# One layer of a hybrid decoder trunk: index queries of rows 64 to 255 alone, index keys in passes of 512 columns

## The chip, the core and the metric

The kernel runs on one core of a Trainium2 chip, as one launch. The metric is the device time of that launch in microseconds (us), as the median of several executions. One more execution was taken with the hardware profiler; all rows of the profile come from it.

## The reference, cut to what matters

One layer works on x (256 rows, 1024 features). After an RMS norm, one projection gives the inputs of a convolution branch and of an attention branch whose keys are chosen by an index:

```python
n = RMSNorm(x)
c_a, c_g, q, k, v, qi, ki, wi, gc, ga = split(n @ w_in)   # qi 8 heads x 64, ki 64, wi 8
# index: per block of 128 query rows
logits = einsum('qhd,sd->qhs', qi, ki) * 64**-0.5
score  = einsum('qh,qhs->qs', wi * 8**-0.5, relu(logits))
score  = where(key <= row, score, -inf)
idx    = top_k(score, 64)              # k_top = min(256, 256 // 4)
s      = q . k[idx], -inf where idx > row ; softmax ; times v[idx]
h = x + W_mix(g_conv * Conv(n) + g_attn * Attn(n))
h = h + CrossAttn(RMSNorm(h), RMSNorm(mem))
h = h + W2 relu(W1 RMSNorm(h))^2 ; final RMSNorm
```

A row r has r + 1 keys that it may look at. Rows 0 to 63 have at most 64 of them, so that the choice of 64 takes all, whatever the scores are. Only rows 64 to 255 need index queries.

## The kernel before

**Number format.** Every large product is made in float32 precision from two parts of each operand: a high part (rounded by ScalarE, `act(hi, raw, Copy)`) and a low part (the rest, `raw - hi`, by VectorE). Three products are kept: high by high, high by low, low by high. The activations of a tile lie as high and low beside each other, 256 columns each. A *wide* tile (`tile_b` with `wide=True`) therefore makes, for each of 8 blocks of features, one pass of 512 columns with the high weights (high and low activations at once) and one pass of 256 columns with the low weights. The two halves of the PSUM bank are then merged: ScalarE copies the second half out, VectorE adds the first (`merge`, L479). A tile that is not wide makes three passes of 256 columns and needs no merge. `back` alternates the order in which neighbouring tiles make their wide and narrow passes.

**Order of the work.** All engines follow one order, written out by the program itself; each engine's queue is first in, first out. `STREAM` lists the weight chunks (1 MB each) in the order of use: four `conv` chunks, two `qi` chunks (four tiles of 128 index query features), `ki` (64 key features and the 8 head weights `wi`, 72 columns), four more `conv` chunks, the gates `gc` and `ga`, then `v`, `q` and `k`, the memory's `xk` and `xv`, then `ao`, `co`, `mix`, the cross attention and the feed-forward part. Chunks are fetched on SyncE's queue into three buffers; a buffer comes free when VectorE has made the second low part.

**The planner.** After every tile of products `tick()` (L373) emits one step of each running chain (generators such as `memory`, `merge`, `index_scores`, `head`, `layer_norm`), then as many *fill* operations as the planner allows, then perhaps one `add_some`. Fill operations are VectorE's convolution taps (31 shifts per tile of 128 channels) and the rounds of the top-64 choice. The planner adds up prices in ns of its own: a pass of n columns costs `pe.total` n/2.4; a VectorE operation costs `dve.total` n/0.96 + 70, or + 125 with a scalar by pointer. It emits fill operations while `dve.total < pe.total - 1000` (L377). When all taps of a tile are out, `settled(t)` adds the tile to `usum` and to `done`; when eight are done, the chain `layer_norm` is started. It makes its first step at the *next* tick. One step per tick it emits the means (`ps_mub`), squares, sums (`ps_vr`), the spread of the root (`ps_rsb`), and then, per pair of channel tiles, a multiplication (VectorE), two Silu and a copy (ScalarE, L912 and L913) and the low part (VectorE, `parts_of`), which comes one step after the copy. Its result `u_p` is the input of `co`, which follows `ao` on TensorE.

**Taps by DMA.** Some taps are made by ScalarE (`products`, L714) and added to `acc` by an accumulating DMA that POOL issues (`add_tap`, L715). `add_some` emits the first one at the first tick after `conv` chunk 3, the next when `pe.total` has grown by a pause of 5000. Each of these DMAs adds into the same region, and each waits on POOL for the one before it to land.

**Index.** `qi_t` holds the four tiles of index queries (features by 256 rows). `ki2` (a part of `picked`) holds the keys twice, `wi_t` the head weights. `index_scores` is started after the key tile: at the tick after the first tile of `conv` chunk 4 it transposes `wi_t` (`ps_wi`) and emits the 16 passes of query block 0 (`ps_idx`), which read rows 0 to 127 of `qi_t` for all four tiles. TensorE reaches them behind that `conv` tile.

**Memory.** The chain `memory` squares the memory rows, has POOL take the root `rs_m` (L629), has TensorE spread it over the partitions (two transposes, `ps_mrb`) for ScalarE to copy into `mrb`, and then splits `mem_t` into parts, one of 8 per tick. `mrb` is used much later, in `residual`.

Of the kernel before, what the change touches and what calls it, by code (L numbers as in the profile page):

```python
# [8 lines left out]
F32 = mybir.dt.float32  # L9
F32R = mybir.dt.float32r  # L10
BF16 = mybir.dt.bfloat16
AF = mybir.ActivationFunctionType
ALU = mybir.AluOpType
# [3 lines left out]
P = 128  # L17
D = 1024
S = 256
KT = D // P  # L20
# [3 lines left out]
HD = 128  # L24
XH = 4
K_TOP = 64
IDX_SCALE = float((8 ** -0.5) * (64 ** -0.5))
ATT_SCALE = float(HD ** -0.5)
NEG_FILL = -1.0e38
NEG_TAKEN = -3.4e38  # L30
NEG_BIAS = -1.0e30
# [23 lines left out]
NK = 72  # L55
# [36 lines left out]
class Parts:  # L92
# [5 lines left out]
    def of(self, part, kt, n):  # L98
        t = self.tiles[kt // 4][:, kt % 4 : kt % 4 + n, part, :]
        return t[:, 0, :] if n == 1 else t  # L100

    def high(self, kt, n=1):
        return self.of(0, kt, n)
# [18 lines left out]
def block_kernel(ctx, tc, x, xt, mem, memt, wst, wki, vecs, convw, gout, out):  # L122
    nc = tc.nc
    ctx.enter_context(tc.manual_schedule())
    pe = Counted(nc.tensor, pe_price)
    dve = Counted(nc.vector, dve_price)
    act = nc.scalar.activation
# [5 lines left out]
    lows = ctx.enter_context(tc.tile_pool(name="lows", bufs=HALVES))  # L133
# [4 lines left out]
    def t8(name, dt=F32, shape=(P, KT, S)):  # L138
        return big.tile(list(shape), dt, tag="t8", bufs=12, name=name)
# [4 lines left out]
    def w2(name, dt=F32, shape=(P, 512)):  # L144
        return work.tile(list(shape), dt, tag="w2", bufs=8, name=name)
# [13 lines left out]
    def ps_aux(name):  # L159
        return bank("aux", 2, name)  # L160
# [3 lines left out]
    def ps_turn(name):  # L164

        mm_turn[0] += 1
        return (ps_mm if mm_turn[0] % 2 else ps_acc)(name)
# [156 lines left out]
    def split_high():  # L324
        if high_jobs and high_jobs[0].here() and (not high_jobs[0].slot or nsplit[0] - nused[0] < HALVES - held[0]):
            job = high_jobs.pop(0)
            nsplit[0] += job.slot
            while job.steps:
                job.step()
            job.high()  # L330
# [9 lines left out]
    nsplit, nused, held = [0], [0], [1]  # L340

    def weights(kind, i, half, kt):

        key = (kind, i, half)
        while key not in prepared:
            split_high()
            split_low()
        nused[0] += key not in elsewhere
        return [w if kt is None else w.rearrange("p (k n) -> p k n", k=kt) for w in prepared.pop(key)]


    chains, fours, fill, turn, done, ended = [], [], [], [0], [], []
# [16 lines left out]
    def split_ahead():  # L369
        split_low()  # L370
        split_high()

    def tick():  # L373
        for c in list(chains):
            if next(c, "end") == "end":
                chains.remove(c)
        while (len(fill) > 1 or (fill and (len(ended) > 5 or nused[0] < 5))) and dve.total < pe.total - 1000:  # L377
            fill_one()
        if fours and next(fours[0], "end") == "end":
            fours.clear()  # L380
        dve.total = max(dve.total, pe.total - 2000)
        add_some()
# [14 lines left out]
    def start(gen):  # L397
        chains.append(gen)
        return gen
# [10 lines left out]
    def mm_b(ps, wh, wl, x2, kt, start, stop):  # L410
        mm3(ps, wh, wl, x2.high(kt), x2.low(kt), start, stop)

    def tile_b(ps, w, x2, kts=range(KT), wide=False, late=False, back=False):

        ps = ps[: w[0].shape[2]]

        def lows(last):  # L420
            for kt in kts:
                pe.matmul(ps[:, S:], w[1][:, kt, :], x2.high(kt), start=False, stop=last and kt == KT - 1)

        if wide and not late:
            for kt in kts:
                pe.matmul(ps, w[0][:, kt, :], x2.both(kt), start=kt == 0, stop=back and kt == KT - 1)
                if back and kt == 0:
                    lows(False)
            if not back:
                lows(True)  # L430
            return
        for kt in kts:
            wh, wl = w[0][:, kt, :], w[1][:, kt, :]
            if not wide:
                mm_b(ps[:, :S], wh, wl, x2, kt, kt == 0, kt == KT - 1)
            elif kt == 0:
                pe.matmul(ps, wh, x2.both(kt), start=True, stop=False)
                pe.matmul(ps[:, S:], wl, x2.high(kt), start=False, stop=False)
            else:
                pe.matmul(ps[:, S:], wl, x2.high(kt), start=False, stop=False)  # L440
                pe.matmul(ps, wh, x2.both(kt), start=False, stop=kt == KT - 1)

    back = [False]

    def is_wide(kind, ct):

        return kind in ("f1", "qi", "gc", "ga", "ao", "xk", "q", "k") or (kind in ("mix", "co") and ct < 6)

    def form_b(kind, i, x2, after, ps_of=ps_mm):

        for ct in range(2):
            w = weights(kind, i, ct, KT)
            if (kind, i, ct) != ("mix", 3, 1):
                split_ahead()
            ps = ps_of(f"ps_{kind}{i}{ct}")
            wide = is_wide(kind, 2 * i + ct)
            tile_b(ps, w, x2, wide=wide, back=back[0])
            back[0] = wide and not back[0]
            after(2 * i + ct, ps if wide else ps[:, :S])
            tick()  # L460
# [24 lines left out]
    def merge_now(dst, ps):  # L485
        for _ in merge(dst, ps):
            pass
# [9 lines left out]
    def copy_to(dst):  # L497
        return lambda ct, ps: copy_out(dst[:, ct, :], ps)
# [27 lines left out]
    picked = w4("picked", F32, (P, D))  # L526
    ki2 = picked[:, 3 * S :]
# [3 lines left out]
    ps = ps_aux("ps_warm")  # L531
# [22 lines left out]
    def spread(cols, name):  # L554

        ps = ps_aux(f"ps_{name}")
        for rb in range(2):
            pe.transpose(ps[:, rb * P : rb * P + P], cols[:, rb : rb + 1].to_broadcast([P, P]), ident)
        return ps[:, :S]


    n2 = parts_t8("n_p")
# [8 lines left out]
    for rb in range(2):  # L571
        for kt in range(KT):
# [5 lines left out]
                             in1=x_rm[:, 1, D // 2 :], scale=1.0 / D, scalar=EPS, op0=ALU.mult, op1=ALU.add,  # L578
# [21 lines left out]
    for lo, hi in ((0, 1), (1, 2), (2, 4), (4, 6), (6, 8)):  # L600
        dve.tensor_tensor(out=n_f[:, lo:hi, :], in0=xg[:, lo:hi, :],
                          in1=rsb_n.unsqueeze(1).to_broadcast([P, hi - lo, S]), op=ALU.mult)
# [10 lines left out]
    rs_m = cst.tile([P, 2], F32, name="rs_m")  # L613
    mrb = cst.tile([P, S], F32, name="mrb")

    def memory():
        mem_rm = t8("mem_rm", F32, (P, 2, D))
        mem_t = t8("mem_t")
        nc.sync.dma_start(mem_rm, mem.rearrange("(r p) d -> p r d", p=P))
        nc.sync.dma_start(mem_t, memt)  # L620
        yield
        yield
        yield
        ss = small.tile([P, 2], F32, tag="ss", name="ss_m")
        for rb in range(2):
            row_square(mem_rm, rb, ss)
            yield
        dve.tensor_scalar(ss, ss, 1.0 / D, EPS, ALU.mult, ALU.add)
        nc.gpsimd.tensor_tensor(out=rs_m, in0=ss, in1=half, op=ALU.pow)  # L629
        yield  # L630
        act(mrb, spread(rs_m, "mrb"), AF.Copy)
        for kt in range(KT + 1):
            if kt < KT:
                act(mem2.high(kt), mem_t[:, kt, :], AF.Copy, scale=g_mem[:, kt : kt + 1])
            if kt > 0:
                j = kt - 1
                dve.scalar_tensor_tensor(out=mem2.low(j), in0=mem_t[:, j, :], scalar=g_mem[:, j : j + 1],
                                         in1=mem2.high(j).bitcast(F32), op0=ALU.mult, op1=ALU.subtract)
            yield


    u = t8("u")
# [123 lines left out]
            start(memory())  # L766


    qi_t = t8("qi_t", F32, (P, 4, S))
    for i in range(2):  # L770
        form_b("qi", i, n2, copy_to(qi_t), ps_turn)
    wk = weights("ki", 0, 0, KT)
    split_ahead()
    ps = ps_mm("ps_ki")
    tile_b(ps, wk, n2)
    for j in range(2):
        act(ki2[j * 64 : j * 64 + 64, :], ps[:64, :S], AF.Copy)
    wi_t = w2("wi_t", F32, (P, S))
    act(wi_t[64:NK, :], ps[64:NK, :S], AF.Copy, scale=IDX_SCALE)
    tick()  # L780
    wi = cst.tile([P, 2, 8], F32, name="wi")

    bias = [picked[:, :P], picked[:, P : 3 * P]]
# [6 lines left out]
    def choose(qb, score):  # L790

        def turn(r):
            def go():
                m8 = small.tile([P, 8], F32, tag="m8", name=f"m8_{qb}_{r}")
                dve.max(out=m8, in_=score)
                dve.match_replace(out=score, in_to_replace=m8, in_values=score, imm_value=NEG_TAKEN)
                dve.total += 250
            return go

        def mask():  # L800
            dve.tensor_scalar(bias[qb], score, -3.3e38, NEG_BIAS, ALU.is_gt, ALU.mult)
            causal(bias[qb], qb, NEG_BIAS)

        return [turn(r) for r in range(K_TOP // 8)] + [mask]

# [417 lines left out]
    dst = open_banks("xo")  # L1223
    w = weights("xo", 0, 0, 1)
# [9 lines left out]
    w = weights("xo", 0, 1, 1)  # L1234
# [259 lines left out]
    for c in range(JOINED):  # L1494
        hidden.append(Hidden(c + 2))
        x, later = hidden[c], hidden[c + 2]
        wide = c in WIDE
# [134 lines left out]
```

## Time and profile before

| | |
|---|---|
| median of 3 runs | 497.05 us (496.95 to 497.06) |
| the profiled execution's own time | 497.16 us |
| its span in the profile | 495.0 us |
| TensorE (PE) busy | 487.3 us, 98% |
| VectorE (DVE) busy | 460.5 us, 93% |
| ScalarE (ACT) busy | 378.4 us, 76% |
| GpSimd (POOL) busy | 50.6 us, 10% |
| TensorE clock granted | 0.998 |

Times in the rows are us from the start of the span. PE is a matmul pass, PEld its weight load, SP the engine that issues most DMAs. A busy TensorE counts passes that overlap in its pipeline, so that the distance between the starts of two passes in a row, not the length of one, is what a pass costs.

### The profile page before, as it was taken

How to read it: one execution, taken by the hardware profiler on the slowest of the kernel's cores; microseconds unless marked ns; L12 is line 12 of the kernel's file. 1: busy time of each engine (PE TensorE's matmuls, PEld its weight loads, DVE VectorE, ACT ScalarE, POOL GpSimd, SP SyncE). 2: the span in 40 equal slices, each digit the busy share in tenths (PEclk: the TensorE clock that was granted, in tenths of full speed). 3: DMA queues.
4: the chain of work that ended last, by engine and by line, in shares of the span. 5: the costliest groups of instructions: out<-in, count | busy, mean ns of one | idle time of the engine just before them, and what ended most of it. 6: DMA issues, size and time to landing. Idle time of an engine off the chain costs nothing.

```text
span 495.0 us, 7793 instructions
## 1 busy us (share of the span) xinstructions
PE 487.3 (98%) x2832; PEld 429.2 (87%) x2832; DVE 460.5 (93%) x828; ACT 378.4 (76%) x678; POOL 50.6 (10%) x67
## 2 busy tenths in 40 slices
PE   8999999999999999999999999999999999999995
PEld 7888888888888889888889999988998888888884
DVE  4999999999999989989988987899999999999986
ACT  5778879999887786767846558687777878888852
POOL 2002212221111211000000000000010101121000
PEclk9999999999999999999999999999999999999999
DMA  8958676989887977354645552866979879999802
GB/s 318 354 215 276 180 190 198 304 245 253 277 219 223 246 176 213 115 171 175 250 169 183 209 204 87 290 189 138 253 274 292 237 242 262 294 333 314 256 9 85
DMA packets 33430, 110.36 MB, mean 223 GB/s; under 512 B 11104, under 2 KB 13408, under 8 KB 24432
## 3 DMA queue, kind: packets, MB, share of 16 engines
q1 hardware_dynamic: 24416, 93.03, 54.4%
q0 software_dynamic: 8688, 16.64, 17.2%
q8 instruction: 22, 0.36, 0.3%
q10 hardware_dynamic: 288, 0.20, 0.1%
q14 instruction: 16, 0.13, 0.1%
HBM read 99.29 MB, written 1.05 MB: 203 GB/s over the span
## 4 chain that ended last, share of the span: by engine, by line
PE 97%; DVE 1%; issue 0%; ACT 0%; DVEq 0%
PE ps_f L87 18%; PE ps_p L87 15%; PE ps_conv L87 9%; PE ps_co L87 5%; PE ps_mix L87 5%; PE ps_ao L87 5%; PE ps_k L87 5%; PE ps_ga L87 5%; PE ps_gc L87 5%; PE ps_q L87 5%; PE ps_v L87 4%; PE ps_xo L87 3%; PE ps_xq L87 2%; PE ps_xk L87 2%; PE ps_qi L87 2%; PE ps_xv L87 2%
## 5 line engine op out<-in xcount | busy, mean ns | idle before, releaser
L87 DVE TENSOR_TENSOR lo<-raw,hi 128x1024 fp32r<-128x1024 f32 x133 | 161.3, 1215 | 2.5 <-ACT hi L315 2.2
L315 ACT ACTIVATE hi<-raw 128x1024 fp32r<-128x1024 f32 x133 | 138.5, 1048 | 6.2 <-DMA raw<-in_wst_dram 6.1
L87 PE MATMUL ps_f<-ff_p,hi 128*128 128x512 f32 (+1 forms) x320 | 72.4, 347 | 0.0
L87 PEld LDWEIGHTS ps_f<-ff_p,hi 128*128 128x128 f32 x320 | 56.2, 189 | 8.2 <-ACT ft L1344 0.3
L87 DVE SCALAR_TENSOR_TENSOR acc<-u,cw,acc 128x241 f32<-128x241 f32 (+23 forms) x142 | 58.5, 465 | 0.1
L87 PE MATMUL ps_f<-ff_p,lo 128*128 128x256 f32 x256 | 46.8, 282 | 0.0
L87 PEld LDWEIGHTS ps_f<-ff_p,lo 128*128 128x128 f32 x256 | 39.3, 191 | 1.8
L715 POOL DMA_DIRECT2D acc<-products x25 | 21.7, 880 | 124.2 <-ACT products L714 59.5
L87 PE MATMUL ps_conv<-n_p,hi 128*128 128x512 f32 x112 | 29.2, 397 | 0.0
L87 PEld LDWEIGHTS ps_conv<-n_p,hi 128*128 128x128 f32 x112 | 20.4, 188 | 4.4 <-issue 0.3
L714 ACT ACTIVATE products<-u,cw 128x243 f32<-128x243 f32 (+19 forms) x50 | 22.1, 492 | 0.0
L293 ACT ACTIVATE inner<-sums 128x1024 fp32r<-128x1024 f32 x13 | 13.8, 1060 | 10.5 <-DVE sums L87 10.5
L87 DVE TENSOR_TENSOR ft<-ft 128x128 f32<-128x128 f32 (+2 forms) x49 | 19.4, 397 | 1.1 <-ACT ft L1344 0.6
L683 ACT ACTIVATE ring<-u,cw 128x236 f32<-128x236 f32 (+10 forms) x44 | 20.2, 480 | 0.0
L87 PE MATMUL ps_p<-outer,fs 128*128 128x512 f32 x78 | 20.1, 393 | 0.0
L87 PE MATMUL ps_v<-hi,n_p 128*128 128x512 f32 x64 | 19.9, 389 | 0.0
L87 PE MATMUL ps_p<-inner,fs 128*128 128x512 f32 x78 | 19.8, 389 | 0.0
L87 PE MATMUL ps_co<-u_p,hi 128*128 128x512 f32 (+1 forms) x80 | 19.3, 350 | 0.0
L87 PE MATMUL ps_mix<-mix_p,hi 128*128 128x512 f32 (+1 forms) x80 | 19.2, 349 | 0.0
L87 PE MATMUL ps_k<-n_p,hi 128*128 128x512 f32 x64 | 17.4, 403 | 0.0
L87 PE MATMUL ps_q<-n_p,hi 128*128 128x512 f32 x64 | 17.3, 402 | 0.0
L87 PEld LDWEIGHTS ps_p<-inner,fs 128*128 128x128 f32 x78 | 14.6, 188 | 3.0
(445 smaller groups left out, 1215.0 us busy)
## 6 DMA issues: line engine op xcount, KB each, us to landing
raw<-in_wst_dram SPq DMA_DIRECT2D x67, 1024.0 KB, 5.7
raw<-in_wst_dram SPq DMA_DIRECT2D x28, 512.0 KB, 6.7
sums<-in_wst_dram POOLq DMA_DIRECT2D x15, 512.0 KB, 8.0
acc<-products POOLq DMA_DIRECT2D x25, 256.0 KB, 5.5
x_rm<-in_x_dram SPq DMA_DIRECT2D x2, 512.0 KB, 4.0
mem_rm<-in_mem_dram SPq DMA_DIRECT2D x1, 1024.0 KB, 7.6
mem_t<-in_memt_dram SPq DMA_DIRECT2D x1, 1024.0 KB, 9.6
h_t<-in_xt_dram SPq DMA_DIRECT2D x1, 1024.0 KB, 7.0
```

The costliest lines, as they stand in the source:

```text
L87: return fn(*args, **kwargs)
L293: act(hi, src, AF.Copy)
L315: act(hi, raw[:, ns], AF.Copy)
L683: act(dst[:, t, :], u[:, 4 * g + t, : S - s], AF.Copy, scale=cw[:, 4 * g + t, TAPS - 1 - s : TAPS - s])
L714: act(prod[:, a, s:], u[:, t, : S - s], AF.Copy, scale=cw[:, t, TAPS - 1 - s : TAPS - s])
L715: nc.gpsimd.dma_start(acc[:, ts, :], prod, accum_op=ALU.add)
```

## The change

1. The four `qi` tiles are made by a new function `tile_behind` for rows 64 to 255 alone: wide passes of 2 x 192 = 384 columns and narrow passes of 192. `query_part` merges 192 columns.
2. POOL sets rows 0 to 63 of `qi_t` to zero, and the first 64 rows of the bias of block 0 (`picked`). Both memsets stand behind the `qi` loop, ahead of the key tile. `mask` leaves those 64 rows of the bias alone.
3. The key tile becomes wide: 8 passes of 512 columns and 8 of 256 in place of 24 of 256. It is merged at once into `wi_t`, from which ScalarE then makes `ki2` and the head weights. `back` is turned over behind it, so that all later wide tiles up to `co` alternate the other way round.
4. The spread of the memory's root and its copy to `mrb` move to the end of the chain `memory`, nine ticks later.
5. The planner's distance of 1000 becomes 0 from the tick on at which four tiles are `done`.

```diff
+FREE = K_TOP
+    def behind(self, kt, row):
+        return self.tiles[kt // 4][:, kt % 4, :, row:]
@@ tick
-        while (len(fill) > 1 or (fill and (len(ended) > 5 or nused[0] < 5))) and dve.total < pe.total - 1000:
+        while (len(fill) > 1 or (fill and (len(ended) > 5 or nused[0] < 5))) and dve.total < pe.total - (1000 if len(done) < 4 else 0):
             fill_one()
+    def tile_behind(ps, w, x2, row, back=False):
+        both = ps.rearrange("p (a n) -> p a n", a=2)
+        def lows(last):
+            for kt in range(KT):
+                pe.matmul(both[:, 1, row:], w[1][:, kt, :], x2.high(kt)[:, row:], start=False, stop=last and kt == KT - 1)
+        for kt in range(KT):
+            lo = row
+            pe.matmul(both[:, :, lo:], w[0][:, kt, :], x2.behind(kt, lo), start=kt == 0, stop=back and kt == KT - 1)
+            if back and kt == 0:
+                lows(False)
+        if not back:
+            lows(True)
@@ memory
         yield
-        act(mrb, spread(rs_m, "mrb"), AF.Copy)
         for kt in range(KT + 1):
             ...
             yield
+        act(mrb, spread(rs_m, "mrb"), AF.Copy)
@@ the index queries and keys
-    for i in range(2):
-        form_b("qi", i, n2, copy_to(qi_t), ps_turn)
+    def query_part(dst, ps):
+        both = ps.rearrange("p (a n) -> p a n", a=2)[:, :, FREE:]
+        act(dst, both[:, 1, :], AF.Copy)
+        yield
+        dve.tensor_tensor(out=dst, in0=both[:, 0, :], in1=dst, op=ALU.add)
+    for ct in range(4):
+        w = weights("qi", ct // 2, ct % 2, KT)
+        split_ahead()
+        ps = ps_turn(f"ps_qi{ct}")
+        tile_behind(ps, w, n2, FREE, ct % 2 == 1)
+        start(query_part(qi_t[:, ct, FREE:], ps))
+        tick()
+    assert not back[0]
+    nc.gpsimd.memset(qi_t[:, :, :FREE], 0.0)
+    nc.gpsimd.memset(picked[:FREE, :P], 0.0)
     wk = weights("ki", 0, 0, KT)
     split_ahead()
     ps = ps_mm("ps_ki")
-    tile_b(ps, wk, n2)
+    tile_b(ps, wk, n2, wide=True)
+    back[0] = True
+    wi_t = w2("wi_t", F32, (P, S))
+    merge_now(wi_t[:NK, :], ps[:NK, :])
     for j in range(2):
-        act(ki2[j * 64 : j * 64 + 64, :], ps[:64, :S], AF.Copy)
-    wi_t = w2("wi_t", F32, (P, S))
-    act(wi_t[64:NK, :], ps[64:NK, :S], AF.Copy, scale=IDX_SCALE)
+        act(ki2[j * 64 : j * 64 + 64, :], wi_t[:64, :], AF.Copy)
+    act(wi_t[64:NK, :], wi_t[64:NK, :], AF.Copy, scale=IDX_SCALE)
     tick()
@@ mask
-            dve.tensor_scalar(bias[qb], score, -3.3e38, NEG_BIAS, ALU.is_gt, ALU.mult)
+            rows = slice(0 if qb else FREE, P)
+            dve.tensor_scalar(bias[qb][rows], score[rows], -3.3e38, NEG_BIAS, ALU.is_gt, ALU.mult)
```

## The prediction, made before the changed kernel was timed

> **What bounds the kernel now.** I read the page's busy times first, then what TensorE (PE) waited for, then the chain that ended last, in order of time.
>
> ```profile
> PE 487.3 (98%) x2832; PEld 429.2 (87%) x2832; DVE 460.5 (93%) x828; ACT 378.4 (76%) x678; POOL 50.6 (10%) x67
> PE ps_warm L533 <- DVE zero_r L517: 1.9, 1, 1.9
> ```
>
> PE is the bound, and it waited once, 1.9 us, before its first pass. From there the chain is PE alone until the last products:
>
> ```profile
> 31.96 8.34 PE ps_qi L87 x48
> 40.29 0.38 PE ps_mrb L87 x2
> 40.67 2.80 PE ps_qi L87 x16
> 43.47 2.82 PE ps_ki L87 x24
> 46.29 2.78 PE ps_conv L87 x16
> 49.07 0.22 PE ps_wi L87 x2
> 49.28 1.09 PE ps_idx L87 x16
> ...
> 168.85 0.33 PE ps_pt L87 x3
> ...
> 219.05 0.43 PE ps_mub L87 x2
> ...
> 231.09 0.22 PE ps_rsb L87 x2
> 231.31 11.16 PE ps_ao L87 x64
> 242.47 22.57 PE ps_co L87 x144
> ```
>
> So each pass that goes is worth its distance to the next, and each new wait of PE costs in full. The profiled execution took 497.16 us, 0.11 above the median of the runs, 497.05; I work on the former and take 0.11 off at the end. A measurement of this kernel tells about 0.2% (1.0 us) from no change.
>
> **The narrower queries.** A run of narrow passes and one of wide ones give the prices.
>
> ```profile
> 33.61 1.12 PE L87 MATMUL ps_qi<-n_p,lo 128*128 128x256 f32 x8
> 34.56 0.40 PE L87 MATMUL ps_qi<-n_p,hi 128*128 128x512 f32 x1
> ...
> 35.75 3.59 PE L87 MATMUL ps_qi<-n_p,hi 128*128 128x512 f32 x15
> 39.18 1.11 PE L87 MATMUL ps_qi<-n_p,lo 128*128 128x256 f32 x8
> ```
>
> Start to start, eight narrow passes take 34.56 - 33.61 = 0.95, 0.119 each; 15 wide ones 39.18 - 35.75 = 3.43, 0.229 each. 256 columns thus cost 0.110, 128 cost 0.055. The 32 wide passes lose 128 columns each: 1.76 us. The narrow ones lose 64, which the slope puts at 0.0275, down to 0.091; but a pass of only 128 columns still takes 0.33 / 3 = 0.110 (`ps_pt`), so there is a floor under short passes. A 192-column pass lies between 0.091 and 0.119; the nearest row says 0.110, which saves 32 x 0.009 = 0.28 us (ends 0 and 0.9).
>
> **Keys.** 24 passes took 2.82 us, 0.1175 each. Eight of 512 and eight of 256 columns take 8 x 0.229 + 8 x 0.1175 = 2.77: 0.05 saved. **The root's spread** cost 0.38 where it stands, since its transposes waited for POOL; the like pair `ps_rsb` costs 0.22. It saves 0.38 ahead of the index products and pays 0.22 back later; its nine ticks of delay meet nobody, as `mrb` is read in `residual` only. The other order of wide and narrow passes behind the keys leaves their number as it is: nothing (some 0.1 either way).
>
> Without new waits PE would reach `ps_idx` 1.76 + 0.28 + 0.38 + 0.05 = 2.47 us sooner, at 49.28 - 2.47 = 46.8, and the gain left after the spread is 2.25.
>
> **New wait at the index products: the zeros.** `ps_idx` of block 0 reads rows 0 to 127 of `qi_t`, so it now needs POOL's memset. What stands ahead of that in POOL's queue?
>
> ```profile
> 7.57 0.29 POOL L708 MEMSET products<- 128x248 f32 x1
> 38.20 0.91 POOL L715 DMA_DIRECT2D acc<-products  x1 [30.33 <-ACT products L714]
> 38.84 1.35 POOL L629 TENSOR_TENSOR rs_m<-ss_m,half 128x2 f32<-128x2 f32 x1
> 47.72 0.91 POOL L715 DMA_DIRECT2D acc<-products  x1 [7.53 <-ACT wi_t L779]
> 53.67 0.86 POOL L715 DMA_DIRECT2D acc<-products  x1 [5.04 <-DMA acc<-products]
> ```
>
> The second accumulating DMA stood 7.53 us in front of a closed gate. The releaser named is ScalarE's `wi_t`, which it doesn't read. Its own input was long there, and the first DMA landed just then:
>
> ```profile
> 36.74 0.86 ACT L714 ACTIVATE products<-u,cw 128x236 f32<-128x236 f32 x2
> 41.66 0.87 ACT L714 ACTIVATE products<-u,cw 128x237 f32<-128x237 f32 x2
> ...
> acc<-products POOLq DMA_DIRECT2D x1, 256.0 KB, 9.0
> ```
>
> 38.20 + 9.0 = 47.2, and 0.5 later POOL goes on. Where is the second DMA emitted after the change? The first is emitted at the tick after the first `qi` tile and sets the next due 5000 planner ns later. A `qi` tile now counts 8 x 576 / 2.4 = 1920: after the third it has 3840, after the fourth 5760. So the second DMA goes out at the fourth tile's tick, still **ahead of the memsets**, and the zeros stand behind a wait for the first DMA's landing. The first starts at the same time as before, since ScalarE, busy with earlier work, makes its input at 36.74, two microseconds after the PE tile. If it lands at 47.2 again: second DMA at 47.7, next POOL operation 0.64 behind it (as 38.84 behind 38.20), memset 0.29, done at 48.65; the second memset is read much later. `ps_idx` then starts at 48.7, not at 46.8: PE waits 1.9 us, and of the 2.25 gained 0.35 is left. PE can do nothing else there, its queue is in order.
>
> The landing sets this price alone. Over all 25 of these DMAs, and for the third alone:
>
> ```profile
> DMA to landing us min/median/max: 3.4/5.5/10.0
> ...
> acc<-products POOLq DMA_DIRECT2D x1, 256.0 KB, 3.7
> ```
>
> At 10.0 the kernel is 0.6 slower at this point; at 7.1 or less the zeros come in time (7.1 + 1.5 + 38.2 = 46.8). The weight chunks that compete are fetched when VectorE frees a buffer, and with fewer taps emitted in this stretch that is sooner, so more traffic, not less, meets this DMA. I take 9.0 again.
>
> The merged keys put a VectorE addition into the chain to `wi_t`. From the key tile's last pass (46.29 - 2.47 = 43.8): copy 0.38, addition 0.42, two copies and `wi_t`:
>
> ```profile
> 46.33 0.77 ACT L777 ACTIVATE picked<-ps_ki 64x256 f32<-64x256 f32 x2 [1.23 <-PE ps_ki L87]
> 47.11 0.38 ACT L779 ACTIVATE wi_t<-ps_ki 8x256 f32<-8x256 f32 x1
> 45.94 1.22 DVE L87 TENSOR_TENSOR lo<-raw,hi 128x1024 fp32r<-128x1024 f32 x1
> ```
>
> That is 1.95 with handoffs some 2.3, at 46.1; PE asks at 46.6. If VectorE is inside a weight split of 1.22, PE waits up to 0.7, but that lies under the wait for the zeros: nothing.
>
> **New wait ahead of `co`: one tick.** Fewer planned PE ns mean fewer taps emitted by any given tick: 32 x (128 + 64) / 2.4 = 2560 less, VectorE 70 more (an addition of 337, four merges 67 shorter). The new distance gives 1000 back from the fourth finished tile on; 1630 stays missing. I added up the kernel's own prices in the order of emission: before, at the tick after the third `xv` quarter, `pe.total` is 193,947 and `dve.total` 192,085, and the last two fill operations (337 each, the `usum` additions) go out, the last started at 192,422 under a limit of 192,947. With the change the limit is 193,947 - 2560 = 191,387, and the last would start at 192,492. It misses by 1105, three taps. The remaining fill goes out one tick later, and `layer_norm` makes its first step after the first `ao` tile instead of ahead of it. In the trace its end is tight:
>
> ```profile
> 216.29 0.87 DVE L87 TENSOR_TENSOR usum<-usum,acc 128x256 f32<-128x256 f32 x2
> 240.14 0.68 DVE L87 TENSOR_TENSOR acc<-acc,ps_rsb 128x512 f32<-128x512 f32 x1
> 243.27 0.69 DVE L87 TENSOR_TENSOR u_p<-acc,u_p 128x512 fp32r<-128x512 f32 x1
> ...
> 240.85 1.09 ACT L912 ACTIVATE acc<-acc,vec 128x256 f32<-128x256 f32 x2
> 241.98 0.63 ACT L913 ACTIVATE u_p<-acc 128x512 fp32r<-128x512 f32 x1
> ...
> 244.42 0.28 PE L87 MATMUL ps_co<-u_p,lo 128*128 128x256 f32 x1
> 244.54 0.62 PE L87 MATMUL ps_co<-u_p,hi 128*128 128x512 f32 x2
> ```
>
> The last low part ends at 243.96; PE's seventh wide pass of `co` needs it at 244.54. An `ao` tile with its tick is (242.47 - 231.31) / 4 = 2.79. One tile later the copy ends at 242.61 + 2.8 = 245.4. The low part now follows it at once (before, a weight split lay between): 246.1. PE waits 246.1 - 244.5 = 1.6. Ends: 0 if the shift doesn't come, 2.2 if the low part moves by the whole tile.
>
> **Sum.** -2.25 + 1.9 + 1.6 = +1.25: 497.16 + 1.25 - 0.11 = 498.3. Everything else that is added (mask of fewer rows, VectorE's addition of 0.42) lies on engines that PE doesn't wait for.
>
> **The rivals.**
> *The zeros are in time; only the tick costs.* This needs the first accumulating DMA to land within 7.1 us of its start. For it: the median of the 25 is 5.5, and the third took 3.7. Against it: the one in this place took 9.0 between weight chunks. Time: 497.05 - 2.25 + 1.6 = 496.4, not slower. The Trainium skill, "DMA: Bandwidth & Descriptors", section on the anatomy of one DMA, fits a POOL-issued transfer as 2.0 us plus its bytes over 436 GB/s, which for 256 KB is an estimated 2.6 us; by that rule this rival wins. The row above, 9.0 in this place and never under 3.4, disagrees with the rule, so I trust the row.
> *The zeros cost, the tick does not:* `co` has more room than I read, say because ScalarE, with one step less ahead of it, runs sooner. 497.05 - 0.35 = 496.7.
> *Neither:* the change does what it seems to, 497.05 - 2.25 = 494.8, 494.2 if the narrow passes follow the slope down to 0.091.
> *The narrow passes don't get shorter:* alone it changes nothing, as PE only waits less for the zeros.
>
> **How the numbers follow.** Both waits: 0.60, at 498.3 (own range 497.4 to 499.4, from a landing of 8.5 to 10.0 us and 1.2 to 2.2 at `co`). Tick alone 0.15, zeros alone 0.12, neither 0.13. Leaving out "neither" and the far end of the first case, the range is 495.6 to 499.4. Slower means over 498.0: 0.6 of the first case, 0.36. Faster means under 496.06: most of "neither", a third of "tick alone" and little else, 0.20. Within: 0.44.
>
> **What would show it.** Right: `ps_qi` wide passes start every 0.174 us and narrow ones near 0.110; PE's list of waits has POOL's `qi_t` (1 to 2.5 us) ahead of `ps_idx`, with a memset directly behind a waiting DMA issue; `ps_mub` stands behind the first `ao` tile and PE waits for `u_p` inside `co`. Wrong: the memset is done before the first `conv` tile behind the keys ends, or `ps_mub` still stands ahead of `ao`.

## The result and the profile after

The changed kernel took 500.28 us (median of 14 executions, 498.42 to 508.4), the kernel before 497.12 (14 executions, 496.92 to 502.68). The ratio of the two is 1.0063, with a 95% interval of 1.0035 to 1.009: slower, by more than the 0.2% that can be told. Medians here and below are over all executions; the ratios and their intervals leave out the executions furthest above the rest, and are not the ratios of these medians. The profiled execution took 499.72 us with a span of 497.9 (before: 497.16 and 495.0), and its mean granted clock was 0.994 (before: 0.998).

The page's busy times and TensorE's list of waits (us in total, times, longest) of the changed kernel:

```profile
PE 486.5 (98%) x2824; PEld 428.9 (86%) x2824; DVE 460.8 (93%) x829; ACT 378.8 (76%) x679; POOL 52.7 (11%) x69
PE ps_idx L88 <- POOL qi_t L806: 3.2, 1, 3.2
...
PE ps_mub L88 <- DVE usum L88: 0.2, 1, 0.2
```

TensorE's narrower passes should have taken some 2 us off its busy time; only 0.8 is gone. And one wait of 3.2 us is new. TensorE's timeline of the changed kernel (start, us, group) shows both places:

```profile
33.17 1.03 PE L88 MATMUL ps_qi<-n_p,lo 128*128 128x192 f32 x8
34.04 0.36 PE L88 MATMUL ps_qi<-n_p,hi 128*128 128x384 f32 x1
...
35.11 2.78 PE L88 MATMUL ps_qi<-n_p,hi 128*128 128x384 f32 x15
37.73 1.03 PE L88 MATMUL ps_qi<-n_p,lo 128*128 128x192 f32 x8
...
46.60 0.28 PE L88 MATMUL ps_wi<-ident,wi_t 8*128 8x8 f32 x2
50.13 1.16 PE L88 MATMUL ps_idx<-picked,qi_t 64*128 64x128 f32 x16 [3.25 <-POOL qi_t L806]
51.22 3.68 PE L88 MATMUL ps_conv<-n_p,hi 128*128 128x512 f32 x8
54.74 1.11 PE L88 MATMUL ps_conv<-n_p,lo 128*128 128x256 f32 x8
```

Start to start, 15 wide passes take 37.73 - 35.11 = 2.62, 0.175 each, and eight narrow ones 34.04 - 33.17 = 0.87, 0.109 each. `ps_wi` ends at 46.88, so that TensorE was ready for `ps_idx` 2.40 us sooner than the 49.28 of before. Then it stood 3.25 us. The eight `conv` passes behind that start 3.52 / 8 = 0.44 us apart, where passes of 512 columns had been 0.229 apart.

POOL's timeline says what it stood for:

```profile
38.13 0.91 POOL L735 DMA_DIRECT2D acc<-products  x1 [30.22 <-ACT products L734]
38.77 2.09 POOL L649 TENSOR_TENSOR rs_m<-ss_m,half 128x2 f32<-128x2 f32 x1
48.84 0.91 POOL L735 DMA_DIRECT2D acc<-products  x1 [7.98 <-ACT sg L501]
49.43 0.65 POOL L806 MEMSET qi_t<- 128x256 f32 x1
```

The zeros stand behind the second accumulating DMA, whose issue stood 7.98 us. The chain of work that ended last, of the changed kernel and then of the kernel before (start, length, what), gives the reason and the account:

```profile
38.13 10.17 DMA acc<-products
50.13 1.16 PE ps_idx L88 x16
51.29 10.12 PE ps_conv L88 x48
...
72.31 0.22 PE ps_mrb L88 x2
...
75.31 22.29 PE ps_gc L88 x128
...
221.88 0.70 PE ps_mub L88 x2
222.58 8.37 PE ps_ao L88 x48
...
245.57 22.53 PE ps_co L88 x144
```

```profile
50.38 8.58 PE ps_conv L87 x48
...
72.67 22.29 PE ps_gc L87 x128
94.97 22.29 PE ps_ga L87 x128
```

The first DMA landed at 48.30, and 0.54 later POOL went on. Against before, `ps_idx` starts 50.13 - 49.28 = 0.85 later. The 48 `conv` passes that follow take 10.12 - 8.58 = 1.54 longer. The root's spread adds 0.22, so that `gc` starts 75.31 - 72.67 = 2.64 later, and `co` 245.57 - 242.47 = 3.10 later. Nothing after that gives much back: the span is 2.9 longer.

What made the passes slow? The windows of 1 us give the granted clock (columns: window, its length, TensorE busy with its instructions, clock, DMA share, GB/s):

```profile
50.00:51.00 1.00, 0.87 (x14) 1.00 0.98 401
51.00:52.00 1.00, 1.00 (x8) 0.66 1.06 336
52.00:53.00 1.00, 1.00 (x3) 0.50 0.92 193
53.00:54.00 1.00, 1.00 (x4) 0.50 0.56 111
54.00:55.00 1.00, 1.00 (x6) 0.63 0.06 20
55.00:56.00 1.00, 1.00 (x10) 1.00 0.07 12
```

The clock stood at half from about 51.3 to 54.7: (0.34 + 0.50 + 0.50 + 0.37) / 0.5 = 3.42 us. At half speed that stretch does 1.71 us less work, which is about the 1.54 that the passes lost.

The other executions of the changed kernel point the same way: the one with a mean clock of 0.999 took 498.42, those at 0.996 took 499.21 and 499.35, those at 0.993 and 0.994 took 499.49 to 500.04, and all longer ones had at most 0.992. That is a hint and no more, since only one of them was profiled, and the mean clock also varies from 0.996 to 0.999 between profiles without such a stretch.

### The profile page after: what moved, and what is told of

The parts are those of the page before. It is cut to its first block, busy times and chain, and to the rows that moved or that the text cites. A ratio compares the mean times of both kernels' runs of the same rounds, so it can differ in the third digit from the quotient of the medians.

```text
span 497.9 us, 7783 instructions
## 1 busy us (share of the span) xinstructions
PE 486.5 (98%) x2824; PEld 428.9 (86%) x2824; DVE 460.8 (93%) x829; ACT 378.8 (76%) x679; POOL 52.7 (11%) x69
## 4 chain that ended last, share of the span: by engine, by line
PE 82%; DVE 11%; ACT 2%; DMA 2%; issue 1%; POOL 0%; DVEq 0%; POOLq 0%; ACTq 0%
PE ps_f L88 18%; PE ps_p L88 15%; PE ps_co L88 5%; PE ps_mix L88 5%; PE ps_ao L88 5%; PE ps_q L88 4%; PE ps_ga L88 4%; PE ps_gc L88 4%; PE ps_v L88 4%; PE ps_conv L88 4%; PE ps_k L88 4%; DVE lo L88 3%; DVE acc L88 3%; PE ps_xo L88 3%; PE ps_xq L88 2%; DMA acc<-products 2%
## 5 line engine op out<-in xcount | busy, mean ns | idle before, releaser
L88 DVE SCALAR_TENSOR_TENSOR acc<-u,cw,acc 128x238 f32<-128x238 f32 (+23 forms) x142 | 58.2, 462 | 0.1
L88 PE MATMUL ps_f<-ff_p,lo 128*128 128x256 f32 x256 | 46.8, 282 | 0.0
L88 PE MATMUL ps_conv<-n_p,hi 128*128 128x512 f32 x112 | 30.6, 414 | 0.0
L88 PEld LDWEIGHTS ps_conv<-n_p,hi 128*128 128x128 f32 x112 | 21.4, 197 | 4.7 <-issue 0.3
```

Of the source, the lines that this page charges most:

```text
L88: return fn(*args, **kwargs)
```

## The experiments

All times in us. Each experiment was compared with the kernel before on the same chip; its median was 497.22 beside the first four experiments of the table and 497.14 beside the last four.

| kernel | median | lowest | ratio to before, 95% interval |
|---|---|---|---|
| the change | 500.28 | 498.42 | 1.0063 [1.0035, 1.009] |
| zeros ahead of the queries | 496.74 | 496.27 | 0.9986 [0.9952, 1.0019] |
| second DMA a tick later | 495.62 | 495.19 | 0.9971 [0.9947, 0.9995] |
| zeros first, old distance | 498.15 | 497.90 | 1.0026 [0.9999, 1.0052] |
| 13 unread passes in the stop | 498.84 | 498.36 | 1.0025 [0.9993, 1.0057] |
| 6 unread passes in the stop | 499.25 | 496.53 | 1.0031 [0.9997, 1.0065] |
| second DMA later, keys as before | 495.36 | 494.78 | 0.9975 [0.9949, 1.0] |
| root's spread later, alone | 497.09 | 496.79 | 1.0005 [0.9976, 1.0034] |
| choice rounds priced | 496.79 | 496.64 | 1.0005 [0.9982, 1.0028] |

My theory after the result: the zeros are late because they queue on POOL behind a DMA issue that waits, and the stop of TensorE that follows also lowers its clock. The rivals: the zeros are late for another reason (the memset itself, or TensorE waits for something else there); the slow passes come from something else in that stretch (DMA traffic, for instance) and would be there without the stop.

**Zeros ahead of the queries.** Both memsets stand directly behind the allocation of `qi_t`:

```diff
     qi_t = t8("qi_t", F32, (P, 4, S))
+    nc.gpsimd.memset(qi_t[:, :, :FREE], 0.0)
+    nc.gpsimd.memset(picked[:FREE, :P], 0.0)
...
-    nc.gpsimd.memset(qi_t[:, :, :FREE], 0.0)
-    nc.gpsimd.memset(picked[:FREE, :P], 0.0)
```

> The changed kernel with both memsets of zeros ahead of the query tiles, so that POOL makes them before its first accumulating DMA; nothing else differs. Theory (the zeros queue behind a DMA issue that waits for a landing, and the stop of 3.25 us lets the TensorE clock fall): no wait of TensorE ahead of ps_idx over 0.3 us, the clock at 1.00 behind it, ps_idx at 46.8 us, the whole 2.2 us faster than the kernel before: 494.9, ratio 0.9955. Rival (shorter queries pull weight fetches and vector work together, and that costs the time wherever the zeros stand): 499 or more, with waits of TensorE elsewhere.

It took 496.74 (494.9 expected): 3.5 less than the change, and its interval against before holds 1. The wait for POOL and the low clock are gone (mean clock 0.998). But the full gain did not come. The list of TensorE's waits of this kernel says where a part of it went:

```profile
PE ps_wi L88 <- ACT wi_t L817: 0.8, 1, 0.8
PE ps_ga L88 <- DVE gc_t L88: 0.7, 1, 0.7
PE ps_mub L88 <- DVE usum L88: 0.2, 1, 0.2
```

Together they are 1.7 of the 2.25 that I had expected to be left. They don't account for the median: this profiled execution took 497.33, 0.6 above it, and its span is 0.6 longer than before. By the starts of the tiles its gate stages alone took 1.3 longer than before (45.88 against 44.59 us from the first `gc` pass to the first `v` pass), of which the list shows 0.7. The waits for `gc_t` and `usum` are VectorE running late, at the gates and at the sums.

The first wait was not hidden in the changed kernel, where `ps_wi` comes ahead of the stop and started at 46.60 without one. ScalarE's timeline of the changed kernel and then of this one shows what differs:

```profile
41.13 1.06 ACT L319 ACTIVATE hi<-raw 128x1024 fp32r<-128x1024 f32 x1 [0.88 <-DMA raw<-in_wst_dram]
```

```profile
42.31 1.06 ACT L319 ACTIVATE hi<-raw 128x1024 fp32r<-128x1024 f32 x1 [1.76 <-DMA raw<-in_wst_dram]
```

A weight chunk landed later, and ScalarE, which works in order, came later to the copies of the keys and head weights behind it. In the run with 13 passes it was the same (idle 1.77, wait 0.8).

**Second DMA a tick later.** The memsets stay where the change has them; only the first pause between the accumulating DMAs is longer, so that the second is emitted behind the memsets:

```diff
-    added = [(1, 5000)] * 5 + ...
+    added = [(1, 6500)] + [(1, 5000)] * 4 + ...
```

> The changed kernel with the memsets where they are, and the pause behind the first accumulating DMA raised from 5000 to 6500 planner ns, so that the second one is emitted a tick later, behind the memsets. Theory (it is the waiting DMA issue in POOL's queue): memsets done by 41 to 42 us, no wait ahead of ps_idx, 494.9. Rival (the memset itself waits for the writers of qi_t, or POOL is slow there): the wait stays, 499 to 500.

It took 495.62, 4.7 less than the change, from one number in a list. The profiled execution took 502.41, 6.8 above the median, so for this question only its first 60 us are read. POOL's timeline there:

```profile
40.91 0.30 POOL L806 MEMSET qi_t<- 128x256 f32 x1
...
48.42 0.91 POOL L735 DMA_DIRECT2D acc<-products  x1 [7.07 <-ACT products L734]
```

The memset of `qi_t` is done at 41.21, nine microseconds ahead of the change's, and the DMA still goes out at 48.4. `ps_idx` starts at 47.09, without a wait. (`ps_wi` doesn't wait either, though ScalarE stood 1.83 for its chunk: a tap's `products`, 0.86, had moved behind the keys with the DMA.) It is the order on POOL alone that made the zeros late. The median is 0.7 above the expected 494.9.

Where the rest of this execution's time went can be read too. The list of waits has a stop in the attention stage, and the chain says what came last there:

```profile
PE ps_o L88 <- ACT ptr L994: 4.3, 1, 4.3
```

```profile
177.87 9.91 DMA four<-ring
```

This DMA goes out on POOL behind the accumulating ones. It starts at 177.87 here, where the profiles nearer to their medians have it between 167.1 and 176.0. ScalarE waits for its landing, with TensorE's next input behind it in its queue. With that stop the clock fell as well: it was at half for 6.8 us (0.72 from 188 to 189, 0.50 to 195, 0.86 to 196). The profiled execution with 13 passes, below, shows the same: the DMA starts at 181.77, TensorE stops for 4.1 us, and the clock is at half for 3.4. Why it starts late in these two isn't known.

**Zeros first, old distance.** The zeros are ahead of the queries again, and the planner keeps its distance of 1000 throughout. This is the planner's slip that I had predicted for the change:

```diff
-        ... and dve.total < pe.total - (1000 if len(done) < 4 else 0):
+        ... and dve.total < pe.total - 1000:
```

> The kernel with the zeros ahead of the query tiles, and the planner's distance left at 1000 throughout. The planner's total for TensorE at the tick after the third xv quarter, 192,667 with what the chains emit in that tick, less 1000, lies under 192,492, so layer_norm should begin one tile later. Theory (the tick costs what the prediction said): ps_mub behind the first ao tile, TensorE waits 1.6 us (1.2 to 2.2) for u_p inside co, 496.5. Rival (ScalarE and VectorE catch up): no wait, 494.9, equal to the kernel with the zeros first.

It took 498.15, 1.4 more than with the zeros first alone (1.6 expected; the whole was to be 496.5, but the kernel with the zeros first had missed its own 494.9). In TensorE's timeline of this kernel `ps_mub` now does stand inside the `ao` tiles:

```profile
219.63 1.78 PE L88 MATMUL ps_ao<-o_p,hi 128*128 128x512 f32 x7
221.25 0.60 PE L88 MATMUL ps_mub<-usum,onesd 128*128 128x256 f32 x2
221.50 2.21 PE L88 MATMUL ps_ao<-o_p,hi 128*128 128x512 f32 x8
```

and its list of waits has the two that I had predicted for `co`:

```profile
PE ps_co L88 <- DVE u_p L88: 0.6, 2, 0.3
PE ps_co L88 <- ACT u_p L952: 0.3, 1, 0.3
```

These waits sum to 0.9, but the list doesn't show all of the loss: from the first `co` pass to the first `mix` pass it takes 24.27 us (241.87 to 266.14), 1.7 more than the 22.53 with the zeros first alone. So that step costs what I said, where the planner slips. In the changed kernel it doesn't slip.

**Unread passes in the stop.** To the change, 13 passes of 512 columns are added between `ps_wi` and `ps_idx`, into a bank that nobody reads. TensorE then works while it waits:

```diff
+        ps = ps_aux("ps_warm2")
+        for j in range(13):
+            nc.tensor.matmul(ps, n2.high(0)[:, :P], n2.both(0), start=True, stop=True)
         for qb in range(2):
```

> The changed kernel with 13 extra passes of 512 columns, whose result nobody reads, between ps_wi and ps_idx: 3.0 us of work in the time in which TensorE waits for the zeros. Theory (the stop lets the clock fall, and the passes behind it cost double for some 3 us): the zeros come as late as before, ps_idx at 50 us, the wide passes behind it 0.23 us apart in place of 0.44, the whole 1.5 us faster than the changed kernel, 498.2. Rival (the passes behind the stop are slow for another reason, or the zeros alone cost it all): no gain, 499.7 to 500.3.

It took 498.84 (498.2 expected), 1.4 less than the change, with work added. The profiled execution took 504.6, with the stop in the attention stage named above; TensorE's timeline around the index:

```profile
47.83 3.25 PE L852 MATMUL ps_warm<-n_p 128*128 128x512 f32 x13
51.00 1.16 PE L88 MATMUL ps_idx<-picked,qi_t 64*128 64x128 f32 x16
52.09 2.11 PE L88 MATMUL ps_conv<-n_p,hi 128*128 128x512 f32 x8
54.04 1.12 PE L88 MATMUL ps_conv<-n_p,lo 128*128 128x256 f32 x8
```

The eight passes behind `ps_idx` take 54.04 - 52.09 = 1.95, 0.24 each, where the change needed 3.52. `ps_idx` starts 0.87 later than in the change, since the head weights came 0.8 late and the passes then took 3.2 us, and the median is still lower.

**Six unread passes.** The same edit with `range(6)`, which leaves a stop of some 1.3 us.

> The changed kernel with 6 in place of 13 extra passes, so that TensorE works 1.4 us more and then stands still for some 1.8 us, not 3.25, ahead of ps_idx. Theory (only a stop as long as the whole one lets the clock fall): as with 13 passes, 498.8, passes behind ps_idx 0.23 us apart. Rival (any stop of over a microsecond lets it fall): passes 0.44 us apart for some microseconds, 500.3 as in the changed kernel.

TensorE's list of waits, and the clock in windows of 2 us:

```profile
PE ps_idx L88 <- POOL qi_t L806: 1.3, 1, 1.3
```

```profile
50.00:52.00 2.00, 1.95 (x20) 1.00 1.01 352
52.00:54.00 2.00, 2.00 (x14) 1.00 0.93 199
```

A stop of 1.3 us leaves the clock at 1.00, beside about as much traffic (352 GB/s) as in the change, so traffic is not what made the passes slow. `ps_idx` starts within 0.1 us of where the change starts it, so that in this stretch the two differ by the length of the stop and the clock behind it. The profiled execution took 498.04, 1.7 less than the change's. The median, 499.25, says less: the 12 executions spread from 496.53 to 504.53, six of them above 499.8, and what those six lost isn't known.

**Second DMA later, keys as before.** The longer pause and, besides, the old key tile with three passes of 256 columns and no merge (the other lines of the key tile as before the change):

```diff
-    tile_b(ps, wk, n2, wide=True)
-    back[0] = True
-    merge_now(wi_t[:NK, :], ps[:NK, :])
+    tile_b(ps, wk, n2)
```

> The kernel with the second accumulating DMA behind the zeros, and the key tile as it was before the change (24 passes of 256 columns, no merge, order of passes not turned). Theory (the merge puts VectorE and three copies of ScalarE between the key tile and ps_wi, and makes VectorE wait for the key tile, 0.6 us idle, which TensorE meets again in the ga stage, where VectorE is the slower one): no wait of TensorE for wi_t, a shorter or no wait in the ga stage, 495.0, some 0.6 faster than with the merged keys (495.6). Rival (the wait in the ga stage comes from the rounds of the choice alone): 495.3, only the wait for wi_t gone. Second rival: the merge costs nothing, 495.6.

At 495.36 it has the lowest median of all, 1.8 under before, with an interval that reaches 1.0. Against the version with merged keys the difference, 0.26, is within what the two intervals leave open. Its list of waits, and two pieces of its chain in the gate stage:

```profile
PE ps_conv L88 <- DMA raw<-in_wst_dram: 0.9, 1, 0.9
PE ps_ga L88 <- DVE gc_t L88: 0.7, 1, 0.7
```

```profile
80.74 0.34 DVE gc_t L88
...
83.65 0.33 DVE gc_t L88
```

The first wait lies at the start of the kernel and costs nothing against before (`ps_conv` begins at 7.79 here and at 7.84 before). There is no wait for `wi_t`, but the version with merged keys had none in its profile either; there ScalarE was done with `wi_t` at 46.82, just as TensorE came, and here at 45.10. So the unmerged keys give room, and no run shows that they saved time. The wait in `ga` is still there: VectorE needs 2.91 us per gate tile, TensorE 22.29 / 8 = 2.79.

**Choice rounds priced.** The rounds of the top-64 choice are dearer than the planner counts. This version adds their missing price (`dve.total += 440 if qb else 310` in place of 250) and sets the distance from the fourth tile on to -1600, on top of the last one.

> The kernel with the unmerged keys, and the planner's prices of the choice rounds raised to what the rows show (a round of 128 keys by 60, one of 256 keys by 190 planner ns), with the distance at -1600 from four finished tiles on, so that layer_norm still begins ahead of ao. Theory (in the gc and ga stages two rounds per tile make VectorE take 2.91 us for a tile that TensorE makes in 2.79, and TensorE meets that as its wait in ga): no wait of TensorE in ga, 494.7, 0.3 to 0.5 faster than with the unmerged keys alone. Rival (the fill put off comes back as waits later): 495.0 or more, with waits in xk, xv or ao.

The wait in `ga` went, as the chain shows, and the list of waits shows what came for it:

```profile
92.75 22.29 PE ps_ga L88 x128
```

```profile
PE ps_mub L88 <- DVE usum L88: 1.6, 1, 1.6
```

`ga` starts 94.97 - 92.75 = 2.22 sooner than before, the whole gain. But what was put off came late at the sums, as the rival said, and 496.79 is 1.4 worse than without the price (494.7 expected). The price and the distance changed together, so the run doesn't tell which of them did it. VectorE, 93% busy, took back a part of what TensorE gained in each version that gained time (waits of 0.2 to 1.6 us for it).

**Root's spread later, alone.** The kernel before, with `act(mrb, spread(rs_m, "mrb"), AF.Copy)` behind the loop of `memory`.

> The kernel before with one part of the change alone: the spread of the memory's root at the end of its chain. Theory: two transposes cost 0.22 in place of 0.38 us, 0.16 saved, and ScalarE no longer waits 0.9 us for them; 497.0, ratio 0.9997. Rival: the delay lets ScalarE wait later instead, no change or 0.2 slower.

497.09 against 497.14: too small to be told from nothing, as expected.

## Why the prediction was wrong

I had said 498.3, in a range of 495.6 to 499.4; it was 500.28. By its own steps:

- **The narrower queries: right.** 0.174 and 0.110 a pass were predicted, 0.175 and 0.109 came. The reason for the 0.110 is weaker than the number: its row, `ps_pt`, holds plain float32 transposes, and the `ps_idx` passes in the same list, also of 128 columns but with 64 rows of weights, take 1.09 / 16 = 0.068 each. So no single floor holds for 128 columns, and that the value fitted 192 columns is in part luck. With the keys and the spread, TensorE was ready for `ps_idx` at 46.88 (predicted 46.8), and the spread cost its 0.22 later.
- **The wait for the zeros: right in its mechanism, too small.** The step "I take 9.0 again" failed: the landing took 10.17, and 9.6 to 10.3 in the five other versions whose profile wasn't far off their median. I had seen that fewer taps bring more traffic, and said so, but gave it no price: from 38.2 to 47.2 us the DMA engines moved 292 and 281 GB/s in the two kernels with the old query tiles (landing 9.0 and 9.1), and 316 to 328 in all others. Of the 1.48 us that `ps_idx` came later than predicted (50.13 against 48.65), the landing made 1.1. Another 0.3 is a misread row: I let the memset begin 0.64 behind the start of the DMA issue and then take 0.29. Its record does begin 0.59 behind, but the issue runs for 0.91, to 49.75, and the memset ends 0.33 after that. Predicted 1.9, measured 3.25.
- **The clock: not in the prediction.** I priced a stop of TensorE at its own length. After 3.25 us of standing the clock went to half, for 3.4 us, which cost another 1.54. With it filled (13 passes) or shortened to 1.3 us, the passes stayed at 0.23 to 0.24. The Trainium skill, "TensorE: Matmul & The Clock Gate", Part 1, "What's actually happening", gives a rule for it: after an idle window of about 3.4 us the array runs at half rate until it has been busy for as long, and the window runs freely, whenever work begins. The length of the low clock, 3.42 us, agrees. Its start does not, if the rule is taken word for word: the stop of 3.25 us is shorter than such a window, and the half rate came 1.2 us after TensorE had gone on. That a stop of 3.25 us is enough is this trace's, and the trace decides. I hadn't asked what the stop does to the passes behind it. The change's execution at a mean clock of 0.999 took 498.42, next to my 498.3; that is luck, since my sum held a wait ahead of `co` that didn't come.
- **The tick ahead of `co`: wrong.** The rows of the chain have `ps_mub` ahead of `ao`, and TensorE waits 0.2 there, not 1.6. The failed step is "With the change the limit is 191,387 ... It misses by 1105". I read `pe.total` where the tick starts and `dve.total` behind the chains' step. But `tick()` first lets the chains emit a step each, and those of that tick carry transposes and `ps_o` passes of the attention heads, 1280 planner ns by the kernel's own prices. The limit is then 191,387 + 1280 = 192,667, and the last start at 192,492 fits by 175. With the old distance it would miss by 825, and the run with that distance slipped as described. The price of the slip was right: 1.6 predicted, 1.7 there.
- **The rivals.** "The zeros cost, the tick does not" (496.7) is what happened, with a dearer zero: -2.40 + 0.22 for the gain, 3.25 for the wait, 1.54 for the clock, 0.2 at the sums make +2.8, against 2.9 of span. "The zeros are in time" needed a landing within 7.1; the estimate from the Trainium skill, "DMA: Bandwidth & Descriptors", anatomy of one DMA, 2.6 us, was off by four times in this place (10.17). "Neither", at 494.8, is nearly what the longer pause makes of the change: 495.62 and, with the old keys, 495.36.
- **Where I had put nothing:** the chain to `wi_t` costs 0.5 to 0.8 in three of the profiles with merged keys and nothing in the other three, the change's among them. I had named up to 0.7 for VectorE inside a weight split; what delayed it was ScalarE, waiting for a weight chunk. VectorE's lag in `ga`, 0.7 in three of the runs without the stop, I hadn't named.

The two errors on one side (the zeros 1.35, the clock 1.54) and the one on the other (the tick, 1.4) leave the profiled execution 1.4 above my 498.3. It is itself 0.6 under the median; the executions above it have a lower mean clock, but which of them lost time as in the two profiles with a stop in the attention stage isn't known.

## What to carry to other kernels

Before you put an instruction into a queue, list what stands ahead of it that waits: a memset of 0.3 us behind a DMA issue that waited 8 us cost this kernel its whole gain, and one number that moved the DMA behind it gave 4.7 us back. Price a stop of TensorE as long as the ones here (3.25 us and more) with the passes behind it at half clock as well, and if it can't be removed, shorten it or fill it. Where a planner compares two totals, take them where it compares, after everything that the same step has added; and where another engine is 93% busy, expect it to take part of what TensorE gains. And when an execution lies far above the rest, read its profile: here another DMA from POOL, started late, had held up ScalarE and with it TensorE.

## What the runs showed of the hardware

The half clock began 1.2 us after TensorE had gone on, not in the stop: the 16 index passes (50.13 to 51.22) still ran as fast as before, and the eight passes behind them at 0.44 each. A stop of 3.25 us brought it on, one of 1.3 us didn't. The stops of 4.3 and 4.1 us in the attention stage brought it on before TensorE went on, for 6.8 us, twice as long, and for 3.4. On POOL the records of neighbours overlap: a memset of 128 x 256 that took 0.30 us after POOL's root has a record of 0.65 directly behind a DMA issue, but 0.32 of that lie inside the issue's own 0.91. And a 256 KB accumulating DMA took 10.2 us to land where it ran beside weight chunks, and 3.3 at best in the same kernel.
